# A hybrid decoder layer on one core: the first gain vector in two column halves, and four weight sums moved from accumulating transfers to VectorE

## The chip, the cores and the metric

One Trainium2 chip, one core. A kernel is timed by the device time of one execution in microseconds (us), as the median of several runs; lower is better. Beside the timed runs there is one profiled execution, whose trace all rows below come from. Engines: PE is TensorE (matmuls, and PEld its weight loads), DVE is VectorE, ACT is ScalarE, POOL is GpSimd, SP is SyncE, which here only issues transfers.

## The reference

One decoder layer on 512 tokens of width 1024, all in float32. Both norms and the dense part at its end are what the change touches:

```
def rms_norm(x, g):
    y = x * lax.rsqrt(jnp.mean(x * x, axis=-1, keepdims=True) + NORM_EPS)
    return y * g
def swiglu(x, w_gate, w_up, w_down):
    return (jax.nn.silu(x @ w_gate) * (x @ w_up)) @ w_down
...
xn = rms_norm(h, norm_mix[l])
proj = xn @ w_in[l]                      # 1024 -> 3128 columns
y_r = rwkv7_group(proj[..., :R_COLS], ...)   # recurrent mixing, 8 heads
y_n = nsa_group(proj[..., R_COLS:], ...)     # sparse attention, 8 heads
h = h + jnp.concatenate([y_r, y_n], axis=-1) @ w_out[l]
h = h + swiglu(rms_norm(h, norm_ffn[l]), w_gate[l], w_up[l], w_down[l])   # D_FF = 2816
return rms_norm(h, norm_final)
```

## The kernel before

Every float32 matmul is made of three: each operand is split into a high part (a rounded copy, made on ACT, line 149) and a low part (the rest, a subtraction on DVE, line 151), and `mm3` (lines 168 to 170) adds high·high, high·low and low·high. So each weight tile costs one ACT and one DVE instruction of 128x1024 elements before PE can use it, and the third matmul of a product (line 170) is the first that needs the low part of the weights.

**The start.** SP issues the first loads in program order (lines 98 to 106): two column halves of the first 128 tokens of x, then the gain vector norm_mix, broadcast to all 128 partitions (512 KB), then the first half of the first weight tile `raw0`, the next 128 tokens of x, the second half of `raw0`, and the rest. `norm_transposed` treats the first 128 tokens in two column halves: for each half, line 197 multiplies x by the row factor and by the gain. Then PE transposes (line 201), the result is split, and the first projection (`proj_tok`) starts with `mm3`.

**Gate and up.** The FFN's two first matrices are multiplied in 11 blocks q of 256 columns of each. A block is a product of 2x2 blocks by a scheme with seven products instead of eight: rows of the weights are halved, columns are gate and up, and the operands on the weights' side are B11 and B21 (gate's two row halves), B22 (up's second half), and four sums: T1 = gate0 + up0, T2 = T1 + up1, T3 = up0 + up1 (the "third sum"), T4 = T2 + gate1. A class `Weights` prepares one block: the constructor loads gate's halves (lines 145, 146); `load_rest` loads the others; `middle` makes and splits T2 and T1; `end` splits T3 and B22 and makes and splits T4. The loads of `load_rest` go to a tile `t1` (gate0, line 1173), to `b22` (up1, line 1174) and to `t3` (up0, line 1175), all from SP. T1 and T3 are then made by transfers: POOL issues a transfer of up0 that adds to `t1` (line 1177), and one of up1 that adds to `t3` (line 1178). Block 1 alone adds on DVE (lines 1183 and 1191). Even blocks hold t1, t2 and t3 in tiles of the tag "t4" (four buffers), odd ones in one tile of the tag "L". DVE adds t1 and b22 to T2 (line 1184) and b21 to T4 (line 1194).

PE takes the products in the order B11, B21, T2, T1, T3, B22, T4 (`first_products`, `last_products`), and DVE combines each result out of PSUM (lines 1241, 1251, 1254, 1257, 1258, 1261, 1265). The split operands go round two tags, "whi" and "wlo", of two buffers each, and the raw weights round three buffers of "wraw".

**Order.** The program is scheduled before it runs: a planner with costs of its own puts the instructions of each engine into one fixed order, by priority (`tc.high_priority()` puts the weights' work first) and by its own estimate of when inputs are there. On the chip each engine then goes through its list in that order, and an instruction whose input has not come holds up all behind it on its engine. The down projection (line 1296 on) follows in the same manner, with sums in place.

Of the kernel before, what the change touches and what calls it, by code (L numbers as in the profile page):

```python
# [13 lines left out]
OP = mybir.AluOpType  # L14
# [3 lines left out]
S, D = 512, 1024  # L18
# [28 lines left out]
def hybrid_layer(ctx: ExitStack, tc: tile.TileContext, x, positions, norm_mix, w_in, mu_shift, w0, w2, a0, a2,  # L47
                 g2, k_k, k_a, r_k, lnx_w, lnx_b, pe_k, wk1, bk1, wk2, pe_v, wv1, bv1, wv2, w_out, norm_ffn,
                 w_gate, w_up, w_down, norm_final, out):
    nc = tc.nc  # L50
    PE, DVE, ACT, POOL = nc.tensor, nc.vector, nc.scalar, nc.gpsimd
# [16 lines left out]
    def st(shape, tag, bufs=1, dtype=F32):  # L68
        return sb.tile(list(shape), dtype, name=tag, tag=tag, bufs=SB_BUFS.get(tag, bufs))
# [3 lines left out]
    w_in, w_out, w_gate, w_up, w_down = (w.rearrange("l a b -> (l a) b") for w in (w_in, w_out, w_gate, w_up, w_down))  # L73


    def bcast_row(v):
        return bass.AP(tensor=v.tensor, offset=v.offset, ap=[[0, 128], [1, D]])
# [17 lines left out]
    gain = st([128, D], "t4")  # L95
    raw0 = st([128, 2048], "wraw").rearrange("p (k n) -> p k n", n=256)
    w0v = w_in[:, kvw:kvw + 256].rearrange("(k p) n -> p k n", p=128)
    for o in (0, 512):
        nc.sync.dma_start(xt[:, 0, o:o + 512], xf[0:128, o:o + 512])
    nc.sync.dma_start(gain, bcast_row(norm_mix))  # L100
    nc.sync.dma_start(raw0[:, 0:4], w0v[:, 0:4])
    nc.sync.dma_start(xt[:, 1], xf[128:256])
    nc.sync.dma_start(raw0[:, 4:8], w0v[:, 4:8])
    for t in range(2, NT):
# [21 lines left out]
    for g in range(2):  # L126
        nc.sync.dma_start(posci[g * 32:g * 32 + 31], bass.AP(tensor=positions.tensor, offset=positions.offset + 31,
                                                               ap=[[16, 31], [1, 1]]))
# [1007 lines left out]
    class Weights:  # L1136
# [25 lines left out]
        def load_rest(self):  # L1162
            self.b22 = st([128, 2048], "wraw")[:, 0:1024].rearrange("p (k n) -> p k n", n=256)
            if self.q % 2:
                tt = st([128, 4, HK, 256], "L")
                self.t1, self.t2, self.t3 = (tt[:, i] for i in range(3))
            else:
                self.t1, self.t2, self.t3 = (st([128, HK, 256], "t4") for _ in range(3))
            if self.q == 1:
                nc.sync.dma_start(self.t3, self.quarter(w_up, 0))  # L1170
                nc.sync.dma_start(self.b22, self.quarter(w_up, 1))
                return
            nc.sync.dma_start(self.t1, self.quarter(w_gate, 0))
            nc.sync.dma_start(self.b22, self.quarter(w_up, 1))
            nc.sync.dma_start(self.t3, self.quarter(w_up, 0))
            with tc.high_priority():
                POOL.dma_start(self.t1, self.quarter(w_up, 0), accum_op=OP.add)  # L1177
                POOL.dma_start(self.t3, self.quarter(w_up, 1), accum_op=OP.add)

        def middle(self, tag=None):  # L1180
            with tc.high_priority():
# [5 lines left out]

        def end(self):
            with tc.high_priority():
                if self.q == 1:  # L1190
                    DVE.tensor_add(self.t3, self.t3, self.b22)
                self.put("T3", self.t3)
                self.put("B22", self.b22)
                DVE.tensor_add(self.t2, self.t2, self.b21)
                self.put("T4", self.t2)
# [102 lines left out]
    halves = [(hid4[a // 4], hid4[b // 4]) for a, b in GROUPS]  # L1298
# [32 lines left out]
    for n, (a, b) in enumerate(GROUPS):  # L1331
        one, two = halves[n]
        a11, a21, a12, a22 = (h[:, :, x] for h in (one, two) for x in (left, right))
        lead, end = n == 0, n == 1
        t1, t2 = block4(a, 0, "wraw"), block4(b, 1, ("gin", "kB")[n])
        t3 = st([128, 4, 512], "wraw") if lead else None
        t3 = [t3[:, 2 * i:2 * i + 2] if lead else st([128, 2, 512], "t4") for i in range(2)]
        for i in range(2):
            nc.sync.dma_start(t3[i], down(a, 1)[:, 2 * i:2 * i + 2])
        t2s.append(t2)  # L1340
        DVE.tensor_sub(a21, a22, a21)
        multiply(m1, a_side(a11), b_side(t1), lead, end)
        DVE.tensor_add(a11, a21, a11)
        with tc.high_priority():
            for i in range(2):
                h = slice(2 * i, 2 * i + 2)
                DVE.tensor_add(t1[:, h], t1[:, h], t3[i])
                POOL.dma_start(t3[i], down(b, 1)[:, h], accum_op=OP.add)
            DVE.tensor_add(t2, t2, t1)
        multiply(m5, a_side(a21), b_side(t1), lead, end)  # L1350
        multiply(m6, a_side(a11), b_side(t2), lead, end)
        DVE.tensor_sub(a21, a11, a22)
        multiply(m7, a_side(a21), b_side(t3), lead, end)
# [30 lines left out]
    for t, banks in accumulate(*jit(lambda k: hid[PLAIN[k]]), w_down, 6, None, [PLAIN[k] * 128 for k in (0, 2, 4)], held, rest):  # L1384
        xo, o = x2[:, t], o2[:, t % 2]
# [49 lines left out]
```

## Time and profile before

| what | value |
|---|---|
| timed runs, median (lowest to highest) | 745.86 us (743.71 to 747.25), 3 runs |
| the profiled execution's own time | 746.93 us |
| its span, first to last instruction | 745.2 us |
| TensorE's mean granted clock, share of full | 0.983 |
| PE busy | 720.3 us, 97% of the span |
| DVE busy | 591.9 us, 79% |
| ACT busy | 402.0 us, 54% |
| POOL busy | 150.8 us, 20% |
| moved by transfers | 85.44 MB, of which 12.58 MB on POOL's queue |

Busy shares are means over stages that have different limits; a matmul counts as busy from its start to its modelled end, so 97% does not say that PE runs at its peak.

### The profile page before, as it was taken

Reading aid. Unit: us, or ns where it says so; the run is one execution under the profiler, and the core shown is the slowest. Engines: PE = TensorE matmul, PEld = TensorE weight load, DVE = VectorE, ACT = ScalarE, POOL = GpSimd, SP = SyncE. Lnnn points to the kernel's source line nnn. Section 1 sums busy time; section 2 is a strip of 40 time slices with the busy share of each in tenths; the row PEclk is TensorE's granted clock in tenths of the full one; section 3 lists DMA queues with packets and bytes.
Section 4 is the critical chain, followed back from the end, with each engine's and each line's share of the span. In section 5 each row is a group of like instructions: output and inputs, shape, how many; then the busy total and the mean of one; then the engine's idle time right before and its main releaser. Section 6 shows DMA issues by size and latency. Waiting matters only on the chain.

```text
span 745.2 us, 14931 instructions
## 1 busy us (share of the span) xinstructions
PE 720.3 (97%) x6045; PEld 627.3 (84%) x6045; DVE 591.9 (79%) x1097; ACT 402.0 (54%) x670; POOL 150.8 (20%) x250
## 2 busy tenths in 40 slices
PE   6999999998989999999999999989999999999996
PEld 6967887898878788777788999989999999777885
DVE  4488778889767998888368999769796899999835
ACT  6388835325267865778438644444453455465414
POOL 3210030228434552354000001211110101000000
PEclk8999999999899999999999999999999999999998
DMA  7623543100044000140320668787868619352402
GB/s 254 200 88 113 168 115 113 58 2 1 2 144 114 3 2 2 34 138 1 111 88 1 157 188 221 185 181 173 213 166 215 143 63 324 122 118 109 142 0 113
DMA packets 71882, 85.44 MB, mean 115 GB/s; under 512 B 4948, under 2 KB 61350, under 8 KB 71814
## 3 DMA queue, kind: packets, MB, share of 16 engines
q1 hardware_dynamic: 60166, 71.91, 29.4%
q0 software_dynamic: 11648, 12.58, 10.9%
q8 instruction: 47, 0.77, 0.4%
q14 instruction: 21, 0.17, 0.1%
HBM read 82.39 MB, written 2.10 MB: 113 GB/s over the span
## 4 chain that ended last, share of the span: by engine, by line
PE 60%; DVE 22%; DMA 7%; issue 5%; ACT 4%; POOL 1%; SPq 0%; DVEq 0%; POOLq 0%; ACTq 0%
PE ps_ra L169 5%; PE ps_ra L170 5%; PE ps_ra L168 5%; PE ps_pj L170 5%; PE ps_pj L168 5%; PE ps_pj L169 5%; DVE wlo L151 4%; PE ps_o L1019 3%; DVE whi L151 3%; PE ps_pj L1010 2%; DVE L L151 2%; DMA L<-in_w_up_dram 2%; PE ps_s L170 2%; PE ps_s L168 2%; PE ps_s L169 2%
## 5 line engine op out<-in xcount | busy, mean ns | idle before, releaser
L149 ACT ACTIVATE whi<-wraw 128x1024 fp32r<-128x1024 f32 (+1 forms) x63 | 62.6, 1030 | 38.9 <-PE ps_ra L170 13.9
L151 DVE TENSOR_TENSOR wlo<-wraw,whi 128x1024 fp32r<-128x1024 f32 (+1 forms) x46 | 55.2, 1227 | 19.2 <-ACT whi L149 14.3
L1007 POOL TENSOR_SCALAR whi<-whi,m,gates 128x128 f32<-128x128 f32 (+3 forms) x64 | 46.3, 758 | 49.5 <-DVE m L1004 40.1
L170 PE MATMUL ps_ra<-L,wlo 128*128 128x512 f32 (+2 forms) x136 | 47.8, 352 | 0.0
L168 PE MATMUL ps_pj<-L,whi 128*128 128x512 f32 (+1 forms) x128 | 44.3, 351 | 0.5 <-DVE t L1261 0.4
L169 PE MATMUL ps_pj<-L,whi 128*128 128x512 f32 (+1 forms) x128 | 44.7, 349 | 0.0
L169 PE MATMUL ps_ra<-L,whi 128*128 128x512 f32 (+2 forms) x128 | 44.1, 344 | 0.0
L168 PE MATMUL ps_ra<-L,whi 128*128 128x512 f32 (+2 forms) x128 | 43.8, 344 | 0.0
L170 PE MATMUL ps_pj<-L,wlo 128*128 128x512 f32 (+1 forms) x128 | 43.2, 337 | 0.1
L1003 ACT ACTIVATE whi<-whi,m 128x128 f32<-128x128 f32 (+3 forms) x64 | 35.5, 556 | 7.2 <-DVE m L1002 6.8
L168 PE MATMUL ps_ra<-whi,L 128*128 128x256 f32 (+1 forms) x108 | 35.3, 330 | 0.5 <-ACT L L149 0.5
L169 PE MATMUL ps_ra<-wlo,L 128*128 128x256 f32 (+1 forms) x108 | 34.8, 323 | 0.2 <-DVE wlo L151 0.2
L170 PE MATMUL ps_pj<-whi,L 128*128 128x256 f32 (+1 forms) x108 | 34.9, 323 | 0.0
L169 PE MATMUL ps_pj<-wlo,L 128*128 128x256 f32 (+1 forms) x108 | 34.8, 322 | 0.0
L168 PE MATMUL ps_pj<-whi,L 128*128 128x256 f32 (+1 forms) x108 | 34.8, 325 | 0.0
L170 PE MATMUL ps_ra<-whi,L 128*128 128x256 f32 (+1 forms) x108 | 34.5, 322 | 0.0
L1002 DVE CUSTOM_DVE_ANT_0 whi<-ps_s,negb 128x128 f32<-128x128 f32 (+3 forms) x64 | 29.4, 484 | 3.0 <-PE ps_pj L1010 2.0
L170 PEld LDWEIGHTS ps_ra<-L,wlo 128*128 128x128 f32 (+1 forms) x136 | 25.1, 184 | 4.1 <-issue 0.5
L168 PEld LDWEIGHTS ps_pj<-L,whi 128*128 128x128 f32 x128 | 24.0, 188 | 4.3 <-DVE t L1261 0.8
L170 PE MATMUL ps_s<-L,whi 128*128 128x256 f32 (+1 forms) x88 | 26.2, 299 | 1.3 <-DVE whi L151 1.3
L1177 POOL DMA_DIRECT2D t<-in_w_up_dram x6 | 8.0, 1331 | 94.8 <-DVE b L1103 58.5
L170 PEld LDWEIGHTS ps_pj<-L,wlo 128*128 128x128 f32 x128 | 24.0, 188 | 3.5 <-DVE wlo L151 0.9
(708 smaller groups left out, 2546.7 us busy)
## 6 DMA issues: line engine op xcount, KB each, us to landing
wraw<-in_w_gate_dram SPq DMA_DIRECT2D x22, 512.0 KB
wraw<-in_w_in_dram SPq DMA_DIRECT2D x9, 1024.0 KB
wraw<-in_w_down_dram SPq DMA_DIRECT2D x9, 1024.0 KB
t<-in_w_up_dram POOLq DMA_DIRECT2D x12, 512.0 KB, 6.1
wraw<-in_w_up_dram SPq DMA_DIRECT2D x11, 512.0 KB
wraw<-in_w_out_dram SPq DMA_DIRECT2D x4, 1024.0 KB
L<-in_w_up_dram POOLq DMA_DIRECT2D x8, 512.0 KB, 6.8
wraw<-in_w_in_dram SPq DMA_DIRECT2D x6, 512.0 KB
```

The lines of the kernel that those rows point to most:

```text
L149: ACT.activation(hi, src, AF.Copy)
L151: (POOL if pool else DVE).tensor_sub(lo, src, hi.bitcast(F32))
L168: PE.matmul(o, lh, rh, start=start, stop=False)
L169: PE.matmul(o, lh, rl, start=False, stop=False)
L170: PE.matmul(o, ll, rh, start=False, stop=stop)
L1002: DVE.tensor_tensor_reduce(pr[:, i], pS[:, i], negb[:, S - n:S], scale=-1.0, scalar=3e38, op0=OP.add, op1=OP.min, accum_out=m[:, i, 0:1])
L1003: ACT.activation(pr[:, i], pr[:, i], AF.Exp, scale=-1.0, bias=m[:, i, 0:1], accum_out=m[:, i, 1:2])
L1007: POOL.tensor_scalar(pr[:, i], pr[:, i], m[:, i, 2:3], gv[:, 1 + b0 + i, h:h + 1], op0=OP.mult, op1=OP.mult)
L1010: PE.transpose(pT[:, j], prr[:, x, j * 128:j * 128 + 128], ident)
L1019: PE.matmul(po[q, 2 * g:2 * g + 2], vtok[:, j % (t + 1), b0 + j // (t + 1), g], pTs[:, par, j], start=False, stop=g == 1 and bs[-1] == 1 a ...
L1177: POOL.dma_start(self.t1, self.quarter(w_up, 0), accum_op=OP.add)
```

## The change

norm_mix is loaded as two transfers of 512 columns each; the second stands behind the first half of the first weights in SP's order. And for the odd blocks 3, 5, 7 and 9 the accumulating transfer of line 1178 is no longer issued; the third sum is made by one DVE addition in `end` (block 1 had this already).

```
-    nc.sync.dma_start(gain, bcast_row(norm_mix))
+    halves = [bass.AP(tensor=norm_mix.tensor, offset=norm_mix.offset + o, ap=[[0, 128], [1, 512]]) for o in (0, 512)]
+    nc.sync.dma_start(gain[:, 0:512], halves[0])
     nc.sync.dma_start(raw0[:, 0:4], w0v[:, 0:4])
+    nc.sync.dma_start(gain[:, 512:D], halves[1])
     nc.sync.dma_start(xt[:, 1], xf[128:256])
     nc.sync.dma_start(raw0[:, 4:8], w0v[:, 4:8])
...
             with tc.high_priority():
                 POOL.dma_start(self.t1, self.quarter(w_up, 0), accum_op=OP.add)
-                POOL.dma_start(self.t3, self.quarter(w_up, 1), accum_op=OP.add)
+                if self.q % 2 == 0:
+                    POOL.dma_start(self.t3, self.quarter(w_up, 1), accum_op=OP.add)
...
         def end(self):
             with tc.high_priority():
-                if self.q == 1:
+                if self.q % 2:
                     DVE.tensor_add(self.t3, self.t3, self.b22)
                 self.put("T3", self.t3)
                 self.put("B22", self.b22)
```

## Rows read from the trace of the kernel before

**Rows 1.** Windows: stretch, length, busy PE, PEld, DVE, ACT, POOL, clock, DMA.
```profile
495.00:500.00 5.00, 3.50 (x31) 3.29 (x29) 2.15 (x3) 0.29 (x1) 1.29 (x1) 1.00 0.56 90
500.00:505.00 5.00, 4.14 (x23) 4.14 (x24) 5.00 (x7) 3.18 (x4) 0.77 (x1) 0.68 1.07 229
...
550.00:575.00 25.00, 25.00 (x220) 25.00 (x219) 19.88 (x22) 10.97 (x12) 2.59 (x2) 1.00 0.77 200
...
580.00:585.00 5.00, 4.22 (x35) 4.22 (x36) 5.00 (x7) 4.17 (x5) 0.87 (x1) 1.00 1.11 233
```

**Rows 2.** Waits of PE from 395 to 610: total us, times, longest.
```profile
PE ps_pj L170 <- DVE wlo L151: 2.4, 1, 2.4
PE ps_ra L170 <- DVE wlo L151: 0.9, 1, 0.9
```

**Rows 3.** Timeline of DVE, gate and up: start, us, instruction, idle before and releaser.
```profile
427.48 1.21 DVE L1191 TENSOR_TENSOR L<-L,wraw 128x1024 f32<-128x1024 f32 x1
428.61 1.21 DVE L1184 TENSOR_TENSOR L<-L,wraw 128x1024 f32<-128x1024 f32 x1
...
475.05 1.23 DVE L1184 TENSOR_TENSOR t<-t,wraw 128x1024 f32<-128x1024 f32 x1 [4.26 <-DMA t<-in_w_up_dram]
...
497.85 1.23 DVE L1184 TENSOR_TENSOR L<-L,wraw 128x1024 f32<-128x1024 f32 x1 [6.97 <-DMA L<-in_w_up_dram]
...
499.59 1.22 DVE L151 TENSOR_TENSOR wlo<-wraw,wlo 128x1024 fp32r<-128x1024 f32 x1
...
536.64 1.23 DVE L1184 TENSOR_TENSOR L<-L,wraw 128x1024 f32<-128x1024 f32 x1 [3.77 <-DMA wraw<-in_w_up_dram]
```

**Rows 4.** Timeline of PE: first use of a B22 low part, blocks 4 and 6.
```profile
500.86 0.39 PE L170 MATMUL ps_pj<-b,wlo 128*128 128x256 f32 x1 [2.37 <-DVE wlo L151]
...
541.13 0.28 PE L170 MATMUL ps_s<-b,wlo 128*128 128x256 f32 x1
```

**Rows 5.** Timeline of POOL: issues of the accumulating transfers.
```profile
456.24 1.30 POOL L1178 DMA_DIRECT2D L<-in_w_up_dram  x1 [6.67 <-issue]
466.07 1.28 POOL L1177 DMA_DIRECT2D t<-in_w_up_dram  x1 [8.53 <-DVE t L1261]
...
481.62 1.29 POOL L1177 DMA_DIRECT2D t<-in_w_up_dram  x1 [4.99 <-DVE whi L151]
491.98 1.30 POOL L1177 DMA_DIRECT2D L<-in_w_up_dram  x1 [9.08 <-issue]
498.14 1.29 POOL L1178 DMA_DIRECT2D L<-in_w_up_dram  x1 [4.85 <-issue]
```

**Rows 6.** Line 1178 over the whole run: its transfers from issue to landing.
```profile
DMA to landing us min/median/max: 5.8/5.8/9.5
```

**Rows 7.** Timeline of SP's queue: loads of blocks 5 and 7.
```profile
479.78 0.37 SPq L1173 DMA_DIRECT2D L<-in_w_gate_dram  x1
...
488.07 0.37 SPq L1174 DMA_DIRECT2D wraw<-in_w_up_dram  x1
...
529.24 0.37 SPq L1174 DMA_DIRECT2D wraw<-in_w_up_dram  x1
```

**Rows 8.** Chain that ended last, 390 to 600: start, us, what.
```profile
436.78 4.69 DMA wraw<-in_w_up_dram
...
450.29 8.39 DMA t<-in_w_gate_dram
```

**Rows 9.** Timeline of the first 12 us, all engines.
```profile
3.48 0.63 ACT L180 ACTIVATE t<-L 128x512 bf16<-128x512 f32 x1 [0.97 <-DMA L<-in_x_dram]
...
4.11 0.63 ACT L183 ACTIVATE t<-L 128x512 bf16<-128x512 f32 x1
...
8.70 1.41 DVE L197 SCALAR_TENSOR_TENSOR b<-L,ss,t 128x512 f32<-128x512 f32 x2 [3.34 <-DMA t<-in_norm_mix_dram]
...
10.13 1.06 ACT L149 ACTIVATE whi<-wraw 128x1024 fp32r<-128x1024 f32 x1 [4.97 <-DMA wraw<-in_w_in_dram]
...
11.22 1.23 DVE L151 TENSOR_TENSOR wlo<-wraw,whi 128x1024 fp32r<-128x1024 f32 x1 [1.00 <-ACT whi L149]
```

More of the change, by code (lines that the diff above doesn't have):

```diff
@@ L99, in hybrid_layer @@
         nc.sync.dma_start(xt[:, 0, o:o + 512], xf[0:128, o:o + 512])
-    nc.sync.dma_start(gain, bcast_row(norm_mix))
+    halves = [bass.AP(tensor=norm_mix.tensor, offset=norm_mix.offset + o, ap=[[0, 128], [1, 512]]) for o in (0, 512)]
+    nc.sync.dma_start(gain[:, 0:512], halves[0])
     nc.sync.dma_start(raw0[:, 0:4], w0v[:, 0:4])
+    nc.sync.dma_start(gain[:, 512:D], halves[1])
     nc.sync.dma_start(xt[:, 1], xf[128:256])
@@ L1177, in load_rest @@
                 POOL.dma_start(self.t1, self.quarter(w_up, 0), accum_op=OP.add)
-                POOL.dma_start(self.t3, self.quarter(w_up, 1), accum_op=OP.add)
+                if self.q % 2 == 0:
+                    POOL.dma_start(self.t3, self.quarter(w_up, 1), accum_op=OP.add)
         def middle(self, tag=None):
@@ L1189, in end @@
             with tc.high_priority():
-                if self.q == 1:
+                if self.q % 2:
                     DVE.tensor_add(self.t3, self.t3, self.b22)
```

## The prediction

> **What bounds the kernel now.** I first read the windows by stage. In a whole stretch of gate and up PE is busy 25.00 of 25.00 us, DVE 19.88 [rows 1]: this stage is bound by PE, and DVE or a transfer matters only where PE is seen to wait. So the next view is PE's waits over the stage. There are two, both on a low part that DVE makes: 2.4 us and 0.9 us [rows 2]. The short windows show what each costs. PE issued 31 and 23 matmuls in the two 5 us after 495; beside the 44 in 5 us of the full stretch (220 in 25) 34 are missing, at 5/44 = 0.114 us each 3.9 us. The wait itself is 2.37 us [rows 4]; the rest is the clock, granted at 0.68 on the mean of the second window, that is at the half level for 64% of it (3.2 us at half speed lose 1.6 us; 2.37 + 1.6 = 4.0). The wait of 0.9 us near 580 is not followed by a lower clock [rows 1]. All there is to win in this stage is therefore 4.0 + 0.9 = 4.9 us.
>
> DVE's timeline tells who is late. The low part that PE wanted (B22 of block 4) starts at 499.59, behind line 1184 of block 5, which stood at the head of DVE's list for 6.97 us until a transfer on tile L landed at 497.85 [rows 3]. In the list of POOL that is line 1177 of block 5, issued at 491.98; it lands 5.87 us later. Why so late? POOL's issues go out at 456.24, 466.07, (one is left out of the rows), 481.62, 491.98 and 498.14 [rows 5]: 6 to 10 us apart, though one keeps POOL for only 1.3 us. At 497.85 DVE is released by the landing [rows 3], and POOL's next issue comes 0.29 us after that. I read this as a chain: an accumulating transfer starts when the one before has landed. So each costs the chain 5.8 to 9.5 us plus 0.3 [rows 6].
>
> **What the change takes from that chain.** Four of its links, line 1178 of blocks 3, 5, 7 and 9. Follow the first. Block 3's goes out at 456.24, and block 4's line 1177 at 466.07. The gate half that the latter adds to was issued at 450.29 and landed 8.39 us later, at 458.68 [rows 8]. Without the link it can go out at 458.7 instead of 466.07: 7.4 us earlier. Line 1184 of block 4, which DVE waited 4.26 us for [rows 3], is then not waited for. What is behind it in DVE's list moves by at most those 4.26 us, among it the read that frees the raw buffer for block 5's loads; I take 3 us, since DVE then meets PE's own pace. Block 5's gate half goes out 3 us before 479.78 [rows 7], line 1177 about 3 us before 491.98 (its two predecessors have moved by more), and t1 is ready at about 494.8 or before, not 497.85.
>
> What is late next is b22, block 5's up half, which line 1184 needs too and whose issue at 488.07 follows a buffer that PE's pace frees, so it stays. Its landing isn't shown there. Bounds: 4.69 us, a load of this size with little beside it [rows 8], so 492.8; and 7.40 us, block 7's, from 529.24 [rows 7] to 536.64, where DVE is released by it [rows 3], so 495.5. I take the middle, 494.2, because fewer bytes are on the way at that time than before, but block 6's loads are.
>
> **What it adds on DVE.** Four additions of 128x1024, each like line 1191 of block 1: 1.21 us, the next instruction 1.13 us behind [rows 3]; 4.5 us in all. DVE's idle time in this stage (5.1 us in 25 [rows 1], some 6.97 of it in one wait) covers them, unless one stands in front of a split that PE waits for. In block 1 line 1191 stands directly before line 1184 [rows 3], so I put it there in the others too. Then from b22's landing to the start of B22's low part it takes 1.13 + 1.74 us (499.59 less 497.85), and it ends 1.22 us after that: 4.09 us. PE wanted it at 500.86 less 2.37 = 498.49, so b22 must land by 494.4. With 494.2 no wait is left; with 495.5 one of 1.1 us is, too short for a lower clock if it goes as near 580; with 492.8 there is room. I charge the middle of 0 and 1.1, rounded down: 0.5 us. If line 1191 falls behind the split instead, it costs nothing. Block 7: line 1184 at 536.64 gives the low part at 536.64 + 1.74 + 1.22 = 539.60, PE uses it at 541.13 [rows 4], so 1.53 us are spare and 1.13 fit. Block 9 loses its 0.9 us of waiting by the same chain; block 3's order is looser.
>
> Sum for gate and up: −(4.0 − 0.5) − 0.9 = −4.4 us (bounds 0 and −4.9). The down projection's loads and splits follow the same tiles as they come free, so I let the gain through whole.
>
> **The start.** The gain vector lets DVE go at 8.70, the first weights let ACT go at 10.13 [rows 9]. Now half a gain vector stands ahead of the weights. First half: the second half of x is used at 4.11, the whole gain at 8.70, so half of it by about 6.4; no earlier than 4.7 (the two halves of x are used 0.63 us apart [rows 9]) and no later than 8.70. Weights: 256 KB fewer ahead of them, by the pace of gain to weights (1.43 us for 512 KB) 0.7 us sooner; bounds 0 and 2.3 (half of 8.70 − 4.11). Second half of the gain: the same bytes ahead of it as ahead of the weights now, so 10.1. DVE then has its multiplication of the second half (0.7 us, half of 1.41), and the weights' low part, now at 11.22, can begin at 10.8 if it stands behind it. So PE's first triple comes 0.4 to 0.7 us sooner: −0.5 us, carried on as PE is busy from there. SP has one more issue of 0.4 us; the transfers queued behind hide it.
>
> That a small transfer has a fixed cost speaks against this half of the change: by the Trainium skill, DMA: Bandwidth & Descriptors, section "Anatomy of one DMA — SWDGE (gpsimd) path", each transfer takes about 2.0 us plus its bytes, fitted for copies from GpSimd. An estimate by that page: two halves cost 2.0 us more than one, and the second comes at 12.1 instead of 10.1. In this trace two half tiles of x that SP issued are used 0.63 us apart, so such costs overlap there; no row shows it for the broadcast gain.
>
> **The sum.** −4.4 − 0.5 = −4.9 us on the profiled execution's 746.93 gives 742.0. The runs' median is 1.07 us below that execution, so I predict 741.0 for the median.
>
> **Rivals** (times for the median; a measurement of this kernel can tell about 0.5%, 3.7 us, from no change).
> *It hides anyway.* The planner keeps block 6's line 1177 ahead of block 5's, or puts another load there, and DVE's head still waits until about 497.8; then the addition is hidden in that wait, the 2.37 us and the clock stay, and only the start's 0.5 us is won: 745.4. For it: the issue that delayed block 5's was block 6's at 481.62 [rows 5], not one that is removed. Against: that one too was held by the chain.
> *The second half of the gain is late.* Its place: the multiplication of the second half stands before the weights' low part in DVE's list. If it lands one gain-to-weights gap behind the present weights, at 10.13 + 1.43 = 11.56, DVE reaches the low part at 12.27 instead of 11.22, 1.05 us lost where I count 0.5 won: 742.5. It decides from 10.5 on. The fixed cost of the Trainium skill's page (DMA: Bandwidth & Descriptors, as above) would make it so.
> *The addition is the new head of DVE's list* (slower). If the planner sets line 1191 before splits that PE needs soon, it waits there for b22. Block 7 has 0.4 us left after the addition; from more than 2 us of such lateness on, a wait like that at 500 with its fall of the clock comes, 4.0 us a time. In blocks 5, 7 and 9: 0 + 4.0 + 3.1 (where 0.9 was) − 0.5 = +6.6: 752.5. For it: block 7 waited 3.77 us for b22 already. Against: line 1184 waits for the same b22 there, so only the addition's own 1.13 us are new.
>
> **How the numbers follow.** Forecast 0.55, hidden anyway 0.27, late gain 0.06, new head 0.12. Faster by over 0.5% is the forecast: 0.55. Hidden anyway and late gain (0.45% faster) lie within 0.5%: 0.33. Slower: 0.12. The forecast's own range is 738.7 to 742.1: its upper end is 1.1 us left at block 5 and nothing won at the start; its lower one the full 4.9 us, and weights 2.3 us sooner at the start. The range for 8 in 10 takes in the hidden case with its spread and leaves out the slower one and a tail below: 738 to 747. The planner may also reorder other stages on so small a cause; I give that no value of its own.
>
> **What would show it.** Right: POOL's issue for block 4 near 459 instead of 466; 16 accumulating transfers instead of 20; no wait of over 1 us of PE in gate and up, and the clock at 1.00 in all its windows; four more additions at line 1191; DVE's first multiplication near 6.5, the first weights' split near 9.4. Wrong: POOL's issues as far apart as before without a transfer between them (then the chain isn't one); line 1184 of block 5 released by t1 at the same time relative to PE; PE waiting on a split behind line 1191; the first weights' low part not before 11.2.

## The result, and the profile after

The changed kernel takes 750.0 us (median of seven runs, 748.79 to 752.98), the kernel before 746.91 us in seven runs on the same chip: the ratio is 1.0059, with a 95% interval of 1.0038 to 1.0080. All ratios here are as recorded, over the runs that stood side by side; they are not quotients of two medians (that would be 1.0041). The forecast was a gain of 0.65%; the change costs 0.6%. The profiled execution took 752.98 us, the longest of the seven, and its span is 751.3 us (before: 746.93 and 745.2 us, beside the median). One run of the experiments (e8, 1161.73 us at a granted clock of 0.559) is in no ratio.

In the changed kernel's lines everything to the first projection stands two further down, gate and up's loads too (1177 is now 1179), the accumulating transfer of t3 is line 1181, and the rest of the block stands three further down (T2's sum 1187, the third sum 1194).

PE's waits in gate and up come first, as total us, times, longest; they answer to [rows 2].

```profile
PE ps_ra L172 <- DVE wlo L153: 5.3, 2, 2.8
PE ps_s L172 <- DVE wlo L153: 2.3, 1, 2.3
PE ps_pj L172 <- DVE wlo L153: 1.1, 1, 1.1
```

8.7 us in four waits stand where 3.3 us in two were. PE's timeline says where; each is the first use of a B22 low part, in the blocks ahead of 3, 5, 7 and 9 (before: [rows 4], and 0.87 us at 580.78).

```profile
463.45 0.39 PE L172 MATMUL ps_ra<-b,wlo 128*128 128x256 f32 x1 [2.79 <-DVE wlo L153]
...
503.68 0.38 PE L172 MATMUL ps_pj<-b,wlo 128*128 128x256 f32 x1 [1.12 <-DVE wlo L153]
...
545.04 0.38 PE L172 MATMUL ps_s<-b,wlo 128*128 128x256 f32 x1 [2.25 <-DVE wlo L153]
...
586.63 0.39 PE L172 MATMUL ps_ra<-b,wlo 128*128 128x256 f32 x1 [2.48 <-DVE wlo L153]
```

The wait that the change aimed at did shrink, from 2.37 to 1.12 us. Three others grew or are new. DVE's timeline, as in [rows 3], tells why:

```profile
459.90 1.22 DVE L1187 TENSOR_TENSOR L<-L,wraw 128x1024 f32<-128x1024 f32 x1 [5.15 <-DMA L<-in_w_up_dram]
461.05 1.22 DVE L1194 TENSOR_TENSOR L<-L,wraw 128x1024 f32<-128x1024 f32 x1
462.18 1.22 DVE L153 TENSOR_TENSOR wlo<-wraw,wlo 128x1024 fp32r<-128x1024 f32 x1
...
499.54 1.23 DVE L1187 TENSOR_TENSOR L<-L,wraw 128x1024 f32<-128x1024 f32 x1 [5.39 <-DMA L<-in_w_up_dram]
500.68 1.22 DVE L1194 TENSOR_TENSOR L<-L,wraw 128x1024 f32<-128x1024 f32 x1
...
502.42 1.21 DVE L153 TENSOR_TENSOR wlo<-wraw,wlo 128x1024 fp32r<-128x1024 f32 x1
...
540.89 1.22 DVE L1187 TENSOR_TENSOR L<-L,wraw 128x1024 f32<-128x1024 f32 x1 [6.52 <-DMA L<-in_w_up_dram]
...
582.49 1.22 DVE L1187 TENSOR_TENSOR L<-L,wraw 128x1024 f32<-128x1024 f32 x1 [5.92 <-DMA L<-in_w_up_dram]
```

In each odd block T2's sum still stands at the head of DVE's list and still waits for t1's accumulating transfer ("<-DMA L<-in_w_up"), 5.15 to 6.52 us. The new addition follows it, 1.13 us, and only then comes the split that PE waits for. In block 3 the order itself is new. Before, the split of block 2's B22 stood ahead of T2's sum, which waited only 1.29 us:

```profile
453.12 1.22 DVE L151 TENSOR_TENSOR wlo<-wraw,wlo 128x1024 fp32r<-128x1024 f32 x1
...
456.22 1.23 DVE L1184 TENSOR_TENSOR L<-L,wraw 128x1024 f32<-128x1024 f32 x1 [1.29 <-DMA wraw<-in_w_up_dram]
```

Now the split stands behind both sums (459.90, 461.05, 462.18).

POOL's timeline shows whether the chain of accumulating transfers became shorter, as [rows 5] had it:

```profile
449.92 1.29 POOL L1179 DMA_DIRECT2D L<-in_w_up_dram  x1 [18.45 <-DVE t L1261]
461.39 1.30 POOL L1179 DMA_DIRECT2D t<-in_w_up_dram  x1 [10.18 <-DVE L L1187]
...
479.86 1.29 POOL L1179 DMA_DIRECT2D t<-in_w_up_dram  x1 [10.62 <-DMA t<-in_w_gate_dram]
492.23 1.29 POOL L1179 DMA_DIRECT2D L<-in_w_up_dram  x1 [11.08 <-DVE b L1270]
499.82 1.30 POOL L1181 DMA_DIRECT2D t<-in_w_up_dram  x1 [6.31 <-issue]
```

It did: block 4's first goes out at 461.39 instead of 466.07. But block 5's, which matters, goes out at 492.23 where it was 491.98, and lands 7.31 us later, at 499.54 (before: 5.87). SP's queue (its loads of blocks 4 and 5, compare [rows 7]) and DVE's list show what it waits for now:

```profile
463.43 0.37 SPq L1147 DMA_DIRECT2D wraw<-in_w_gate_dram  x1
...
480.28 0.37 SPq L1147 DMA_DIRECT2D wraw<-in_w_gate_dram  x1
...
482.01 0.37 SPq L1175 DMA_DIRECT2D L<-in_w_gate_dram  x1
```

```profile
477.89 1.23 DVE L1187 TENSOR_TENSOR t<-t,wraw 128x1024 f32<-128x1024 f32 x1
479.03 1.22 DVE L153 TENSOR_TENSOR whi<-wraw,whi 128x1024 fp32r<-128x1024 f32 x1
...
480.77 1.22 DVE L153 TENSOR_TENSOR wlo<-L,wlo 128x1024 fp32r<-128x1024 f32 x1
```

Block 5's raw loads (480.28) go out 0.03 us after the end of the split of 479.03, which gives a raw buffer back, and the gate half under t1 (482.01) 0.02 us after the end of the split of 480.77, which reads a tile of the same tag L. Both splits stand in DVE's list behind T2's sum of block 4. That sum no longer waits (before: 4.26 us, [rows 3]), but it starts at 477.89 instead of 475.05, because DVE comes late out of block 3. So the gate half goes out 2.23 us later than before (479.78). Block 4's raw load goes out at 463.43, just after the late split of 462.18 has given its buffer back; before, that was at 454.36.

By the trace's landing times the gate half of block 5 landed at 491.55, 9.54 us after its issue, and POOL's issue at 492.23 followed 0.68 us behind; the accumulating transfer before it had landed at 488.63. Before it was the other way round: the gate half had landed at 486.11, the accumulating transfer before at 491.67, and the issue at 491.98 followed 0.31 us behind that. In the changed kernel all eight issues of line 1179 for blocks 3 to 10 come 0.64 to 0.68 us behind the landing of the gate half that they add to. The chain that ended last and POOL's timeline show it for block 9:

```profile
564.21 8.28 DMA L<-in_w_gate_dram
...
573.15 1.29 POOL L1179 DMA_DIRECT2D L<-in_w_up_dram  x1 [10.73 <-DMA L<-in_w_gate_dram]
```

The granted clock, in windows after the first and the last of the four waits (columns as in [rows 1]):

```profile
463.00:468.00 5.00, 4.55 (x39) 4.55 (x40) 5.00 (x8) 2.65 (x3) 0.04 (x1) 1.00 0.98 188
468.00:473.00 5.00, 5.00 (x45) 5.00 (x44) 5.00 (x8) 1.30 (x2) 1.24 (x1) 1.00 1.02 224
...
586.00:591.00 5.00, 4.37 (x37) 4.37 (x38) 5.00 (x7) 3.07 (x4) 0.00 (x0) 1.00 1.13 283
591.00:596.00 5.00, 5.00 (x45) 5.00 (x44) 4.96 (x7) 1.59 (x2) 0.00 (x0) 1.00 0.05 16
```

It stays at 1.00 in the two windows after each of the four waits, and DVE is busy there for 4.96 to 5.00 of 5 us: it is behind and catching up.

The start, from the timeline of the first 12 us, answers to [rows 9]:

```profile
7.69 0.75 DVE L199 SCALAR_TENSOR_TENSOR b<-L,ss,t 128x512 f32<-128x512 f32 x1 [2.19 <-DMA t<-in_norm_mix_dram]
...
8.98 1.06 ACT L151 ACTIVATE whi<-wraw 128x1024 fp32r<-128x1024 f32 x1 [3.68 <-DMA wraw<-in_w_in_dram]
9.72 0.75 DVE L199 SCALAR_TENSOR_TENSOR b<-L,ss,t 128x512 f32<-128x512 f32 x1 [1.28 <-DMA t<-in_norm_mix_dram]
...
10.49 1.22 DVE L153 TENSOR_TENSOR wlo<-wraw,whi 128x1024 fp32r<-128x1024 f32 x1
```

The first multiplication, the weights and the low part all come earlier here, the low part by 0.73 us.

### The profile page after: what moved, and what is told of

It is laid out like the page before. It is cut to its first block, busy times and chain, and to the rows that moved or that the text cites. A ratio compares the mean times of both kernels' runs of the same rounds, so it can differ in the third digit from the quotient of the medians.

```text
span 751.3 us, 14930 instructions
## 1 busy us (share of the span) xinstructions
PE 720.4 (96%) x6045; PEld 626.8 (83%) x6045; DVE 595.8 (79%) x1101; ACT 402.1 (54%) x670; POOL 145.4 (19%) x246
## 4 chain that ended last, share of the span: by engine, by line
PE 61%; DVE 23%; DMA 8%; issue 4%; ACT 3%; POOL 0%; SPq 0%; DVEq 0%; ACTq 0%; POOLq 0%
PE ps_ra L172 5%; PE ps_ra L170 5%; PE ps_ra L171 5%; PE ps_pj L172 5%; PE ps_pj L170 5%; PE ps_pj L171 5%; DMA L<-in_w_up_dram 5%; DVE wlo L153 4%; PE ps_o L1021 3%; PE ps_pj L1012 2%; PE ps_s L172 2%; PE ps_s L170 2%; PE ps_s L171 2%; DVE whi L153 2%; DVE L L153 2%
```

## The experiments

All times stand beside runs of the kernel before on the same chip; ratios carry 95% intervals. "Gate and up" is, in PE's timeline, from the first matmul with 256 moving columns after 400 us to the first with 512 after it; it holds the same 1848 matmuls in every kernel. "Waits" are those of PE on DVE's splits inside it. All columns but the ratio come from one profiled execution, which is not always a typical one: e2's took 756.76 us where its median is 750.04. Each kernel has its own line numbers: in the rows below DVE's split is line 151 or 153 and T2's sum one of 1184 to 1187.

| run | ratio to before | gate and up begin at | take | from there to the end | waits |
|---|---|---|---|---|---|
| before | 1 | 403.19 | 221.96 | 120.05 | 3.3 |
| the change | 1.0059 [1.0038, 1.0080] | 403.94 | 226.97 | 120.39 | 8.7 |
| e1 start only | 0.9994 [0.9973, 1.0015] | 403.80 | 221.22 | 119.68 | 2.5 |
| e2 sums only | 1.0055 [1.0027, 1.0082] | 405.05 | 228.23 | 120.32 | 8.6 |
| e3 no addition | 1.0011 [0.9992, 1.0029] | 402.48 | 222.06 | 119.76 | 2.6 |
| e4 sums only, both behind | 0.9918 [0.9892, 0.9945] | 403.68 | 216.90 | 117.62 | 0.2 |
| e5 third sum behind | 1.0070 [1.0049, 1.0091] | 406.41 | 223.15 | 120.64 | 4.2 |
| e6 before, T2 behind | 0.9924 [0.9904, 0.9944] | 403.87 | 216.40 | 117.63 | 0 |
| e7 the change, both behind | 0.9947 [0.9926, 0.9967] | 404.40 | 217.17 | 117.63 | 0.4 |
| e8 before, T2's sum twice | 1.0062 [1.0042, 1.0082] | 405.00 | 223.06 | 119.24 | 3.6 |
| e9 the same again | 1.0069 [1.0042, 1.0095] | 404.48 | 221.29 | 120.93 | 3.5 |
| e10 T2 behind, twice | 0.9930 [0.9904, 0.9955] | 405.91 | 216.39 | 117.80 | 0 |
| e11 T2's sum twice as long | 1.0055 [1.0030, 1.0080] | 403.90 | 224.32 | 119.78 | 5.1 |
| e12 the change, block 3 behind | 1.0052 [1.0029, 1.0075] | 403.65 | 224.30 | 120.25 | 4.6 |

My first theory was that what costs is work at the head of DVE's list, ahead of B22's split; the rivals were that the transfers taken away moved loads into each other, and that any further work on DVE costs, wherever it stands.

**The change in halves: e1, e2, e3.** e1 has the loads of norm_mix alone, e2 the third sums alone, e3 is e2 with the addition left out in blocks 3, 5, 7 and 9 (so T3 is up0 alone there).

```
 e3:             with tc.high_priority():
                     POOL.dma_start(self.t1, self.quarter(w_up, 0), accum_op=OP.add)
-                    POOL.dma_start(self.t3, self.quarter(w_up, 1), accum_op=OP.add)
+                    if self.q % 2 == 0:
+                        POOL.dma_start(self.t3, self.quarter(w_up, 1), accum_op=OP.add)
...
                 if self.q == 1:
                     DVE.tensor_add(self.t3, self.t3, self.b22)
```

Expected of e1:

> Only the first half of the change: norm_mix in two column halves. Forecast's term: 0.5 us faster, about 746.4 beside the 746.9 of before. Theory from the trace after (gate and up's first rows come 0.4 to 1.0 us later than before): slower by 0.4 to 1.0 us, 747.3 to 747.9, with PE's first transposes at about 7.2 but a second wait for the other half's multiplication near 10 to 11 us.

Expected of e2:

> Only the second half of the change: third sums of the odd blocks on DVE. Theory of the list's head (the addition stands between t1's sum and B22's split, 1.13 us on PE's path in each of four blocks, and block 3's sums now stand before B22's split): PE waits for a low part in blocks 3, 5, 7 and 9, 1.1 to 2.8 us each, 7 to 9 us in all instead of 3.3; time 749 to 750, 2 to 3 us slower. Rival, that the start carries the loss: 746 to 747 or less.

Expected of e3:

> As the sums alone, but blocks 3, 5, 7 and 9 leave the third sum out (T3 is up0 alone): the accumulating transfer is gone and nothing stands in its place. Theory of the list's head: each of the four waits is shorter by 1.13 us, 4.5 us less than with the addition, so 745 to 746.5; block 3 may keep a wait, since t1's sum still stands before B22's split there. Rival, the landing of t1 alone is what got worse: no shorter waits, 749 to 750. The forecast's chain, with the addition as its only flaw: 742 to 743.

The loss is that of the sums: e2 has all of it, e1 none that can be told from no change. In e1's own profile the second half of the gain comes later than in the profile of the whole change, and the low part with it:

```profile
10.78 0.75 DVE L199 SCALAR_TENSOR_TENSOR b<-L,ss,t 128x512 f32<-128x512 f32 x1 [2.68 <-DMA t<-in_norm_mix_dram]
11.55 1.22 DVE L153 TENSOR_TENSOR wlo<-wraw,whi 128x1024 fp32r<-128x1024 f32 x1
```

So one execution gains 0.73 us there and the other loses 0.33 us (11.22 before). e3 says that taking the transfers away is worth nothing (0.1% slower, the interval takes in 0), so the four additions cost about 0.45%, some 3.3 us; the two medians, 750.04 and 748.41 us, are 1.6 us apart. e3 is not the transfers alone: the planner has T2's sum of block 3 ahead of B22's split there too, without any addition, and DVE waits 4.30 us in front of it.

```profile
457.26 1.23 DVE L1185 TENSOR_TENSOR L<-L,wraw 128x1024 f32<-128x1024 f32 x1 [4.30 <-DMA L<-in_w_up_dram]
458.40 1.22 DVE L151 TENSOR_TENSOR wlo<-wraw,wlo 128x1024 fp32r<-128x1024 f32 x1
```

What the transfers are worth with the order held fixed is the comparison of e4 and e6 below.

**The order on DVE: e4, e6, e7.** An instruction is held back by hand until the previous block's B22 is split. e6 does it to T2's sum alone in the kernel before, all transfers kept; e4 to both sums in e2; e7 to both in the whole change.

```
 e6:     split(...):
-            (POOL if pool else DVE).tensor_sub(lo, src, hi.bitcast(F32))
+            last["lo"] = (POOL if pool else DVE).tensor_sub(lo, src, hi.bitcast(F32)).ins
         put(...):
+            last[name, self.q] = last["lo"]
         middle(...):
-                DVE.tensor_add(self.t2, self.t1, self.b22)
+                with tc.issue_after(last["B22", self.q - 1]) if self.q > 1 else nullcontext():
+                    DVE.tensor_add(self.t2, self.t1, self.b22)
```

Expected of e4:

> As the sums alone, but T2's and T3's additions of every block from 2 on are issued only behind the split of the block before's B22. Theory of the list's head: PE's waits on a low part in gate and up fall below 1 us in all, the clock stays full, and the time goes to 742 to 743, below both kernels. Rival, transfers that land too late are the bound themselves: waits of 1 to 3 us come back at T2 of the odd blocks, 747 to 750.

Expected of e6:

> The kernel before with all its accumulating transfers, but T2's sum of every block from 2 on is issued behind the split of the block before's B22. Theory of the list's head: PE's two waits in gate and up vanish, the clock stays full, 742 to 743, and taking the transfers away adds nothing to it. Rival, the shorter chain of transfers is needed as well: waits come back at T2 of the odd blocks, 744 to 746.

Expected of e7:

> The whole change, with T2's and T3's additions issued behind the split of the block before's B22. Theory: as the sums so placed without the start's half, 740.5 to 742; the start adds within 0.7 us either way. Rival, the start's half wins its 0.5 us or loses 1 us steadily: 740.8 or 742.3.

All three beat the kernel before by 0.5 to 0.8%. Gate and up take 216.4 us in e6, 5.6 us less than before, with no wait; the rest is 2.4 us shorter as well (PE's waits there are 1.0 us instead of 2.6; what else shortens it was not followed up). DVE's timeline of e6 at block 5:

```profile
491.85 1.23 DVE L151 TENSOR_TENSOR wlo<-wraw,wlo 128x1024 fp32r<-128x1024 f32 x1 [0.45 <-ACT wlo L149]
496.47 1.23 DVE L1186 TENSOR_TENSOR L<-L,wraw 128x1024 f32<-128x1024 f32 x1 [3.39 <-DMA L<-in_w_up_dram]
```

B22's split begins at 491.85, and T2's sum behind it then waits 3.39 us for the same transfer, which costs PE nothing. With the transfers taken away (e4) it waits less, and now for b22:

```profile
492.17 1.23 DVE L151 TENSOR_TENSOR wlo<-wraw,wlo 128x1024 fp32r<-128x1024 f32 x1 [0.45 <-ACT wlo L149]
494.54 1.23 DVE L1187 TENSOR_TENSOR L<-L,wraw 128x1024 f32<-128x1024 f32 x1 [1.14 <-DMA wraw<-in_w_up_dram]
```

So the shorter chain does bring T2's sum 1.9 us forward, but nobody waits for it any more: e4 is not faster than e6 by anything that can be told. The winning edit is the order, not the transfers.

**One part of the order: e5, e12.** e5 is e2 with only the third sum held back, e12 the whole change with both sums held back in block 3 alone.

```
 e5:     end(...):
-                    DVE.tensor_add(self.t3, self.t3, self.b22)
+                    with tc.issue_after(last["B22", self.q - 1]) if self.q > 1 else nullcontext():
+                        DVE.tensor_add(self.t3, self.t3, self.b22)
 e12:    both sums with  tc.issue_after(last["B22", self.q - 1]) if self.q == 3 else nullcontext()
```

Expected of e5:

> As the sums alone, but only T3's addition of the odd blocks is issued behind the split of the block before's B22; T2's sum stays ahead of it. Theory of the list's head: the same four additions, but each wait of PE is shorter by 1.13 us, so as with no addition at all: 747 to 748.5 and some 4 us of waits. Rival, DVE's load matters wherever the addition stands: 749.5 to 750.5, as the sums alone.

Expected of e12:

> The whole change, with the sums of T2 and T3 behind B22's split in block 3 alone (there the order was split first before the change). If the new order in block 3 is a part of the loss, PE's wait of 2.79 us there goes, block 4's first gate load comes some 8 us earlier again and the waits at blocks 5, 7 and 9 stay within 1 us of 1.12, 2.25 and 2.48: ratio 1.000 to 1.004. If block 3 costs nothing, or its wait only moves into block 5, the ratio is 1.005 to 1.007 as for the whole change.

Both miss what my theory expected. Their profiles do as it says: e5's waits fall from 8.6 to 4.2 us, and in e12 block 3's wait of 2.79 us is gone and block 7's nearly, which leaves 2.09 us at block 5 (501.79), 1.89 us at block 9 (583.67) and 0.6 us of small ones. But the ratios stay at 1.0070 and 1.0052 (medians 750.54 and 748.72 us), about where the rivals had them.

**An addition without the change: e8, e9, e10, e11.** All transfers are kept. In e8 and e9 (one kernel, timed twice) T2's sum is made twice in the odd blocks from 3 on, and the second stands behind B22's split; in e10 T2's sum is behind the split and made twice there; in e11 it is one instruction of twice the length in its old place, whose second half goes to an unused part of the tile.

```
 e8, e9, e10:   DVE.tensor_add(self.t2, self.t1, self.b22)
+               if self.q % 2 and self.q > 1:
+                   DVE.tensor_add(self.t2, self.t1, self.b22)
 e11:
+               if self.q % 2 and self.q > 1:
+                   DVE.tensor_add(self.tt[:, 1:4:2].rearrange("p s k n -> p s (k n)"), twice(self.t1), twice(self.b22))
```

Expected of e8:

> The kernel before with T2's sum made twice in blocks 3, 5, 7 and 9 (the same value again), so four more DVE additions of 128x1024 with every transfer kept; the second one stands behind B22's split in DVE's list. Theory of the list's head: it costs nothing there, 746.5 to 747.5. Rival, DVE is so loaded that any 4.5 us more shows: 750 to 751.5.

The expectations of e9 to e11 count gate and up over a shorter stretch than the table does (179.66 us in the kernel before).

Expected of e9:

> The kernel before with T2's sum made twice in the odd blocks (the second stands behind B22's split on VectorE), timed once more beside a kernel before of its own. Its gate and up took 179.77 us in the first profile against 179.66 us before, so if only work at the head of VectorE's list costs, the time is that of before, ratio 0.998 to 1.003, and what the first timing showed (1.0062) lay in the granted clock of other stages. If every addition on VectorE costs wherever it stands, the ratio is 1.005 to 1.007 again and gate and up grow by about 4 us.

Expected of e10:

> The kernel before with T2's sum behind the split of B22, and made twice there in the odd blocks. If only the head of the list costs, the second sum is free: ratio 0.992 to 0.995, no wait of PE over 0.5 us in gate and up, which take about 170.4 us. If VectorE's load costs wherever it stands, four additions give back 4 to 5 us: ratio 0.997 to 0.999 and gate and up of 174 to 175 us.

Expected of e11:

> The kernel before, all transfers kept, with T2's sum in the odd blocks 3 to 9 made twice as long in one instruction (2048 elements, the second half to an unused place), so that it stands where T2's sum stood: ahead of B22's split in blocks 5, 7 and 9, behind it in block 3. If the addition in that place is what cost the change its time, PE's waits at blocks 5 and 9 grow by 1.1 us each and one may appear at block 7: ratio 1.003 to 1.007, gate and up of 182 to 184 us, with no transfer taken away. If it was the shorter chain of transfers that moved loads into each other, this kernel keeps the time of before, ratio 0.998 to 1.002.

e11 has the loss of the change with no transfer taken away, and its three waits are the two of before, longer, and a new one at block 7:

```profile
PE ps_pj L172 <- DVE wlo L153: 2.7, 1, 2.7
PE ps_ra L172 <- DVE wlo L153: 1.5, 1, 1.5
PE ps_s L172 <- DVE wlo L153: 0.9, 1, 0.9
```

With e3, the rival of colliding loads falls. e8 and e9 contradict the narrow form of my theory: an addition behind the split costs as much, 1.0062 and 1.0069. And e10 contradicts the rival that DVE's load costs wherever it stands: the same four additions cost nothing (0.9930, e6 has 0.9924) once T2's sum is off the head, or nothing beyond the intervals of some 0.25% either way. DVE at block 5, in e9 and then in e10:

```profile
497.43 1.22 DVE L1184 TENSOR_TENSOR L<-L,wraw 128x1024 f32<-128x1024 f32 x1 [6.03 <-DMA L<-in_w_up_dram]
...
499.17 1.22 DVE L151 TENSOR_TENSOR wlo<-wraw,wlo 128x1024 fp32r<-128x1024 f32 x1
500.30 1.22 DVE L1186 TENSOR_TENSOR L<-L,wraw 128x1024 f32<-128x1024 f32 x1
```

```profile
493.89 1.23 DVE L151 TENSOR_TENSOR wlo<-wraw,wlo 128x1024 fp32r<-128x1024 f32 x1 [0.45 <-ACT wlo L149]
499.01 1.23 DVE L1186 TENSOR_TENSOR L<-L,wraw 128x1024 f32<-128x1024 f32 x1 [3.90 <-DMA L<-in_w_up_dram]
...
500.76 1.21 DVE L1188 TENSOR_TENSOR L<-L,wraw 128x1024 f32<-128x1024 f32 x1
```

In e9 the second sum (500.30) runs while the list is late behind T2's wait, so it delays all that follows. In e10 DVE idles 3.90 us in front of T2's sum as well, but with B22's split already done.

**Where e8 and e9 lose: e13 to e16.** Two more profiles of the kernel before and two of e8's kernel, in turn on one chip; the code of each is as above.

Expected of e13:

> The kernel before, profiled again, for the spread of its stages: from gate and up's first product to down's first, 219 to 222 us (221.96 us in the first profile), to the first product 402 to 406 us, down to the end 119 to 121 us.

Expected of e14:

> The second sum of T2 behind B22's split, profiled again. If it is free, gate and up take as long as in the profiles of the kernel before taken beside it, within 1 us, and what is longer lies ahead of the first product or in down. If the second sum costs, gate and up are 3 to 5 us longer than beside it, in PE's waits or in stretches at half clock after them.

Expected of e15:

> As the first further look at the kernel before: gate and up 219 to 222 us.

Expected of e16:

> As the first further look at the second sum of T2: within 1 us of the kernel before in gate and up if it is free, 3 to 5 us longer if it costs.

| | time | gate and up begin at | take | to the end | waits |
|---|---|---|---|---|---|
| e13 before | 749.25 | 405.21 | 222.84 | 119.45 | 3.8 |
| e15 before | 744.97 | 402.27 | 221.35 | 119.58 | 2.4 |
| e14 sum twice | 747.49 | 403.46 | 221.20 | 120.84 | 3.0 |
| e16 sum twice | 750.80 | 404.78 | 223.92 | 120.40 | 5.1 |

With the profiles already taken, the means of the kernel with the sum twice (four profiles) and of the kernel before (three) are 749.1 and 747.1 us; gate and up take 222.4 and 222.1 us, the waits 3.8 and 3.2 us, the rest 120.4 and 119.7 us, and the stages ahead, where both have the same instructions in the same order, end at 404.4 and 403.6 us. The profiles hold less than half of what the ratios show (0.0065 of 746 is 4.9 us), and no one stage holds it. Part of that can be the choice of executions: the three profiles of the kernel before mean 747.1 us, while its runs beside e8 and e9 have medians of 745.37 and 745.64 us. Of the waits, the one at block 5 shrinks (at most 0.63 us in the four profiles, 2.03 to 2.54 before), one at block 7 is new (0.74 to 1.59), and the one at block 9 grows (1.44 to 3.48, before 0.35 to 1.30), most of all in e16:

```profile
540.67 0.38 PE L170 MATMUL ps_s<-b,wlo 128*128 128x256 f32 x1 [1.43 <-DVE wlo L151]
...
583.09 0.58 PE L170 MATMUL ps_ra<-b,wlo 128*128 128x256 f32 x1 [3.48 <-DVE wlo L151]
```

That an addition costs while T2's sum is at the head, and not when it is behind, is shown by the ratios of e8 and e9 against e10. Through which waits it costs the rest stays open.

## Why the prediction was wrong

**The bound was read rightly.** Gate and up is bound by PE: without waits it takes 216.4 us (e6), and the kernel before lost 5.6 us in it, where the prediction counted 4.9. The two waits of [rows 2] and the clock behind the first were all there was to win in this stage, and e6 wins them, with 2.4 us after the stage on top, which "I let the gain through whole" did not foresee.

**The chain of accumulating transfers is there.** In the kernel before it held block 5's issue (landing 491.67, issue 491.98), as forecast, and in the changed kernel the next one still goes out 0.28 us after the sum that a landing releases (499.54, 499.82). With four links fewer, POOL's issue for block 4 comes 4.7 us earlier (461.39) where the forecast had 7.4 (458.7); in e3 it is 459.17.

**The step that failed is "What is behind it in DVE's list moves", with "I take 3 us", and so "Block 5's gate half goes out 3 us before 479.78".** DVE's wait at block 4 did go, but the idle time had moved to block 3: there DVE stood 5.15 us in front of T2's sum, with B22's split behind it, and came to block 4's sum 2.84 us later than before, not 3 us earlier. The reads that free block 5's buffers are behind that sum, so the gate half went out at 482.01, landed at 491.55, and held the issue for t1 in place of the chain. In e3, where no addition was in the way but block 3 has the same new order, it went out at 480.25, though gate and up began 0.71 us earlier there. From the issue of the gate half to the start of T2's sum it took 18.07 us before, 17.53 in the changed kernel and 17.29 in e3: the link taken away was worth 0.5 to 0.8 us, not 3. With the order held by hand and DVE not late (e4) the gate half goes out at 479.62, 0.16 us earlier (gate and up began 0.49 us later there). e3's ratio of 1.0011 says the same in time: "It hides anyway" was right on the transfers in its outcome, not in its reason, since block 6's transfer had landed at 485.11 there and block 5's issue came at 490.40. "Block 9 loses its 0.9 us of waiting by the same chain" failed too: in the kernel before, block 9's issue (567.84) already stood 0.68 us behind the landing of its gate half (567.16), and not behind a link.

**"What is late next is b22"** was therefore not reached. t1 stayed the releaser in all four odd blocks of the changed kernel. b22's 494.2 was a good figure, as e4 shows (494.54, released by wraw), but for an order that the kernel did not have.

**The addition was mis-sized.** I placed it rightly, directly beside T2's sum and ahead of the split, and charged 0.5 us once. The four cost about 3.3 us (e2 against e3). At block 7 "1.53 us are spare and 1.13 fit" supposed that T2's sum starts with b22 at 536.64; it started with t1 at 540.89. At block 3, which I called looser, the order changed, and the split there now stands behind 5.15 us of idle time; that also moved block 4's raw load 9 us back. The rival "The addition is the new head of DVE's list" comes nearest to what happened: right in its place, wrong in the transfer waited for (t1, not b22) and in its price (8.7 us of waits without any fall of the clock, where it had 4.0 us a time). I also took DVE's idle time for cover (the 5.1 us are of the stretch from 550 to 575, the wait of 6.97 us lies outside it); but in these blocks 5.15 to 6.52 us of it lie in one piece in front of T2's sum, and behind that DVE has next to none for 10 us.

**The start** was forecast at −0.5 us; e1's interval, 2.0 us faster to 1.1 us slower, holds that, and no change too. The gain's first half was used at 7.69 and 7.34 where I had 6.4, the second at 9.72 and 10.78 where I had 10.1. By the estimate from the fixed cost that the Trainium skill gives (DMA: Bandwidth & Descriptors, "Anatomy of one DMA — SWDGE (gpsimd) path") the second would have come at 12.1; both profiles have it earlier, though the halves are used 2.03 and 3.44 us apart, not 0.63 us as the halves of x that I went by.

**Shown and open.** Shown by taking it away (e6, e10) is that T2's wait at the head of DVE's list, ahead of B22's split, is what cost the kernel before its waits in gate and up, and what made the additions dear. Shown by e3, and with the order held fixed by e4 against e6, is that the transfers were worth nothing that can be told. Open is how additions that stand behind the split cost 0.6 to 0.7% in the ratios while the profiles show less than half of it; that DVE is late there and passes the delay on is my reading of its timeline.

## What to carry to other kernels

Where a bound engine waits for a split and the splitting engine stands idle in front of another instruction, look first at the order of the two: moving the waiting one behind costs no work and here won 0.8%, while shortening what it waits for won nothing. Idle time of an in-order engine is cover only for work that can run inside it; work that came behind the stall cost here, by the ratios, about as much as its own time. Before a transfer's earlier landing is counted, follow the load under it through its own queue back to the instruction that frees its buffer, and ask whether that instruction moves as well; here it stood in the list of the engine that had become late.

## What the runs showed of the hardware

Waits of PE of the same length are not followed by the same clock. After 2.37 us before the granted clock was 0.68 in the next window, and after 1.77 us in e3 it was 0.66:

```profile
500.00:505.00 5.00, 4.45 (x24) 4.45 (x25) 5.00 (x7) 2.89 (x5) 0.00 (x0) 0.66 1.08 239
```

After 2.79, 2.25 and 2.48 us in the changed kernel it stayed at 1.00 in the windows behind. In these profiles the longer wait was not always the dearer one.

With four of them fewer, the accumulating transfers of 512 KB did not land faster at the two blocks followed here: 5.87 us before and 7.31 us after at block 5, 7.65 us before and 9.98 us after at block 3 (449.92 to 459.90).

In gate and up of all 18 profiles, 296 accumulating transfers in all, none went out before the one ahead of it had landed; the next followed 0.31 us behind at the soonest, and each took 5.71 to 10.76 us from issue to landing. The profile names no semaphore for that wait ("<-issue" in [rows 5]), so what holds it is not shown.

The stages ahead of gate and up, with the same instructions in the same order, ended between 402.3 and 405.2 us in three profiles of the kernel before alone. Differences of 1 or 2 us between two single profiles say little about a change.
